# Fox gate sums from 64 keys to a partition, and low parts on GpSimd at the start of the feed-forward network

## The chip, the cores and the metric

One core of one Trainium2 chip runs the whole program. The time is that of one execution on the device, in microseconds. The engines are TensorE (PE, matmuls), VectorE (DVE), ScalarE (ACT), GpSimd (POOL) and SyncE (SP). In this kernel SP does no arithmetic: it issues every DMA, one after the other, in a fixed order.

## The reference

The reference is one step of a hybrid encoder layer: 1024 rows of a new stream (prompt) and 16 new rows for each of 8 running streams (decode), 1152 rows of width 1024 in all. Cut to what the change touches:

```python
logf = log_sigmoid(fg + fox_b_f)                      # one gate per row and head, 4 heads
fcum = cumsum(logf, axis=1)                           # prompt
fcum = cumsum(concat([past_fox_logf, logf]), axis=1)  # decode: 1024 cached gates, then 16 new
s = q @ k.T * 64 ** -0.5 + (fcum_q[:, None] - fcum_k[None, :])
p = softmax(where(k_pos <= q_pos, s, -inf))           # fox attention
...
hdn = silu(u @ w_gate) * (u @ w_up)                   # FFN, 1024 -> 2816
h = h + hdn @ w_down
```

Fox is one of three mixers that run side by side (stick-breaking attention, fox attention, a state-space scan). An output projection, a cross attention, the FFN and a final norm follow. Everything is float32.

## The kernel before

A float32 product is made of three matmuls of rounded parts. Every operand is split in a high part, rounded by ACT (`ACT.copy` into float32r), and a low part, the difference of the operand and its high part. The low part is made by DVE, or by POOL in pieces of 256 columns (`pool_tt`, L132).

**Order.** The program emits the work as interleaved generators. In the first half `pipeline` takes attention rows, and `fill_s` feeds projections, then `fox_sums`, between them. The framework's scheduler then sets the order on each engine by its own estimate of times. Each engine works its list in order, and SP's list holds all the DMAs.

**Fox sums.** `fox_sums` makes the new gates `lf` (a softplus, L396 to L411, 36 columns) and the prefix sums over the prompt (`fqc`, L676 to L680, with a matmul against a triangle of ones at L678). For decode it loads the cached gates with the key index on the partition: 128 partitions, 64 runs of 4 floats each (L666). It puts them in another order (L683), makes sums over the eight blocks of 128 keys (L693 to L696) and then fifteen matmuls of 128x32 by 128x128 (L708, L710), whose result, 32 rows (stream and head) by 1024 keys, goes through ACT (L711) to a scratch tensor in DRAM (L718), together with the 16 new gates' sums. Later each group of cached fox rows loads one scratch row to each partition (L909), and `fqs` takes the new gates' sums from it (L1246).

**Neighbours of the fox sums.** Cached keys come in pairs of 256 KB loads (`load_k`, L882) into a ring of four tiles `wr`, which the loads of `w_in` (L315) share. PE transposes them (L888), ACT copies them into `kf` (L890), and PE uses them at L873. ACT's cast L290 makes the high parts of `w_in`, POOL's L132 (`wl`) the low ones. Stick-breaking rows go through a DVE scan (L519) and a POOL product (L132, `ws`) before PE transposes them (L925, L577).

**FFN.** Gate and up projections are made tile by tile (22 tiles of 128 columns) as seven products of combined factors instead of eight plain ones. `left_factors(kt, eng)` loads the weights of one tile and makes the seven left factors, each with a high and a low part of 128x512 (`hi_lo`, L1689 on ACT, L1693 on DVE or L132 on POOL). `right_factors` makes the right factors of a group of rows from the transposed rows `u`: `put` writes high (L1753) and low part, and `sub` (L1697) is a difference on DVE, partly in place in `u`. Group 0 has 256 columns, and group 1 has 320 and is made in four pieces, one for each `kp`. At the start `gate_up` runs tile 0 on group 0, tile 1 on group 0, tile 1 on group 1, tile 0 on group 1, and then each further tile on both; `gen1` holds the left factors of tile 1. From tile 2 on, the low parts are on POOL. PE's FFN matmuls are at L1849, DVE's sums of results in PSUM at L1824.

## Time and profile before

| | us |
|---|---|
| median of 3 runs (lowest, highest) | 1916.93 (1914.52, 1922.89) |
| profiled execution | 1915.89 |
| its span | 1914.2 |
| busy: PE, DVE, ACT, POOL | 1837.6, 897.1, 823.7, 622.6 |

A row of the timeline has start, length, engine, line, operation, and what is written from what, with shapes. In square brackets stand the idle time of the engine before it and what ended this. "L882" is line 882 of the kernel before. The granted clock is that of PE as a share of full speed. The profiled execution took 1.7 us more than its span.

### The profile page before, as it was taken

To read this page: it belongs to the slowest core of one execution; us is meant where nothing else is said; L and a number is where in the kernel's file an instruction comes from. 1 tells how busy PE (TensorE), PEld (TensorE's weight loads), DVE (VectorE), ACT (ScalarE), POOL (GpSimd) and SP (SyncE) were. 2 spreads that over 40 slices of the span, in tenths; PEclk is the share of its full clock that TensorE was granted. 3 is DMA by queue.
4 is the path that set the end of the run, shared out by engine and by line. 5 is a ranking of instruction groups with operands and counts; after the bars stand their busy time and mean duration, and the time that the engine had idled before them with its cause. 6 is when DMAs were issued, how large, how long until landed. Compare 5 with 4: busy or idle time off the path is not lost. (4 is left out here: it accounts for less than half of the span.)

```text
span 1914.2 us, 32508 instructions
## 1 busy us (share of the span) xinstructions
PE 1837.6 (96%) x12146; PEld 1641.4 (86%) x12146; DVE 897.1 (47%) x1823; ACT 823.7 (43%) x1782; POOL 622.6 (33%) x921
## 2 busy tenths in 40 slices
PE   7989989999998889999999999999999999999998
PEld 5889877888876667898998889999999999888886
DVE  3421323457646873353445387333333433455554
ACT  6431534545566771243433275333333333344443
POOL 7532416254324563211102205544444443000000
PEclk9999998999999999999999999999999999999999
DMA  9455645536579887244558124322323223567572
GB/s 336 142 165 159 211 115 152 154 109 185 166 220 282 280 290 260 103 150 145 176 194 291 66 91 111 80 70 70 95 74 75 70 70 100 190 194 237 177 246 92
DMA packets 309742, 305.70 MB, mean 160 GB/s; under 512 B 89996, under 2 KB 261108, under 8 KB 309584
## 3 DMA queue, kind: packets, MB, share of 16 engines
q1 hardware_dynamic: 309584, 303.62, 51.6%
q8 instruction: 96, 1.57, 0.3%
q14 instruction: 62, 0.51, 0.1%
HBM read 229.31 MB, written 74.24 MB: 159 GB/s over the span
## 5 line engine op out<-in xcount | busy, mean ns | idle before, releaser
L132 POOL TENSOR_TENSOR wl<-wr,wh 128x256 fp32r<-128x256 f32 (+2 forms) x184 | 138.6, 787 | 222.4 <-ACT wh L290 202.0
L326 PE MATMUL psd<-act,wh 128*128 128x384 f32 x576 | 198.7, 345 | 5.1 <-DVE sg L453 2.7
L327 PE MATMUL psd<-act,wh 128*128 128x384 f32 x576 | 197.6, 343 | 0.0
L328 PE MATMUL psd<-act,wl 128*128 128x384 f32 x576 | 196.8, 342 | 0.7 <-POOL wl L132 0.7
L1849 PE MATMUL pst<-bT,tr 128*128 128x256 f32 (+1 forms) x1068 | 155.0, 293 | 0.0
L1849 PEld LDWEIGHTS pst<-bT,tr 128*128 128x128 f32 x1068 | 144.9, 188 | 0.1
L328 PE MATMUL psd<-wh,act 128*128 128x512 f32 (+3 forms) x424 | 135.8, 322 | 0.0
L326 PE MATMUL psd<-wh,act 128*128 128x256 f32 (+3 forms) x414 | 133.0, 324 | 2.4 <-ACT pt L1445 1.2
L1849 PE MATMUL psd<-bT,tr 128*128 128x320 f32 (+1 forms) x912 | 133.2, 295 | 0.8 <-DVE tr L1693 0.5
L327 PE MATMUL psd<-wl,act 128*128 128x256 f32 (+3 forms) x414 | 132.8, 322 | 0.5 <-POOL wl L132 0.5
L1849 PEld LDWEIGHTS psd<-bT,tr 128*128 128x128 f32 x912 | 124.7, 188 | 1.8 <-DVE tr L1693 0.7
L326 PEld LDWEIGHTS psd<-act,wh 128*128 128x128 f32 x576 | 109.1, 189 | 8.7 <-DVE sg L453 3.1
L132 POOL TENSOR_TENSOR tr<-u,tr 128x256 fp32r<-128x256 f32 x110 | 81.9, 774 | 102.3 <-ACT tr L1689 85.1
L328 PEld LDWEIGHTS psd<-act,wl 128*128 128x128 f32 x576 | 108.9, 189 | 2.3 <-POOL wl L132 1.0
L327 PEld LDWEIGHTS psd<-act,wh 128*128 128x128 f32 x576 | 109.0, 189 | 1.5 <-issue 1.1
L132 POOL TENSOR_TENSOR ws<-ws 128x256 f32<-128x256 f32 (+2 forms) x100 | 68.5, 713 | 115.3 <-DVE ws L519 99.9
L1824 DVE TENSOR_TENSOR tr<-tr,pst 128x256 f32<-128x256 f32 (+1 forms) x86 | 38.6, 449 | 139.5 <-ACT tr L1821 106.3
L251 POOL TENSOR_SCALAR sm<-sm 128x1 f32<-128x1 f32 (+2 forms) x27 | 7.1, 261 | 296.6 <-ACT y L1932 208.0
L132 POOL TENSOR_TENSOR tr<-raw,tr 128x256 fp32r<-128x256 f32 x94 | 69.2, 765 | 84.5 <-ACT tr L1689 76.3
L1689 ACT CAST tr<-tr 128x384 fp32r<-128x384 f32 (+1 forms) x70 | 37.7, 538 | 121.1 <-DMA tr<-hidsc 104.3
L290 ACT CAST wh<-wr 128x512 fp32r<-128x512 f32 (+2 forms) x90 | 52.2, 621 | 80.7 <-PE psd L328 31.0
L326 PEld LDWEIGHTS psd<-wh,act 128*128 128x128 f32 x414 | 78.3, 189 | 9.9 <-ACT pt L1445 1.5
(620 smaller groups left out, 4714.0 us busy)
## 6 DMA issues: line engine op xcount, KB each, us to landing
u<-w_down SPq DMA_DIRECT2D x40, 512.0 KB
raw<-w_down SPq DMA_DIRECT2D x26, 512.0 KB
st<-qksc SPq DMA_DIRECT2D x48, 256.0 KB
wr<-w_in SPq DMA_DIRECT2D x44, 256.0 KB
tr<-hidsc SPq DMA_DIRECT2D x57, 192.0 KB
hidsc<-tr SPq DMA_DIRECT2D x34, 288.0 KB
qksc<-sg SPq DMA_DIRECT2D x48, 192.0 KB
wr<-cache_sb_k SPq DMA_DIRECT2D x32, 256.0 KB
```

The source lines that it names most:

```text
L132: POOL.tensor_tensor(out=out[:, a0:a1], in0=in0[:, a0:a1], in1=in1[:, a0:a1], op=op)
L251: POOL.tensor_scalar(v, ss, inv, EPS, ALU.mult, ALU.add)
L290: ACT.copy(hi, raw)
L326: PE.matmul(out, ah, bh, start=start, stop=False)
L327: PE.matmul(out, ah, bl, start=False, stop=False)
L328: PE.matmul(out, al, bh, start=False, stop=stop)
L1689: ACT.copy(hi, src)
L1824: DVE.tensor_tensor(out=at(out, g), in0=at(x, g), in1=ps[g][:, :GW[g]], op=op)
L1849: PE.matmul(dst[g][:, :GW[g]], x[:, ka], y[:, k, :], start=start and k == 0 and m == 0, stop=stop and k == 3 and m == 2, skip_group_check= ...
```

## The change

In `fox_sums` the cached gates are loaded with 64 consecutive keys of one stream on a partition, 256 contiguous floats (16 partitions to a stream). Four scans on DVE, one for each head, sum along the 64 keys. The totals of the partitions are then summed over the earlier partitions of the same stream by a matmul with a mask (`before`, two more selects on POOL) and added. Two more small matmuls give the sums of the new gates and the streams' totals. The scratch tensor is laid out head by stream by key, and the new gates' sums have one of their own (`fn_sc`). The cached rows load it by two DMAs of 64 partitions instead of one of 128.

At the start of the FFN the low part of the right factor `T1`, in the four pieces of group 1, and the seven low parts of tile 1's left factors go from DVE to POOL.

```diff
     mix_sc = dram([8, 2, P, T], F32R, "mixsc")
     o_sc = dram([8, 2, P, T], F32R, "osc")
     fc_sc = dram([4, SEQ], F32, "fcsc")
-    fs_sc = dram([32, 2, PAST + DEC_S], F32, "fssc")
+    fs_sc = dram([4, DEC_B, PAST], F32, "fssc")
+    fn_sc = dram([32, DEC_S], F32, "fnsc")
     ac_sc = dram([72, P], F32, "acsc")
     mk_sc = dram([256, D], F32, "mksc")
     mv_sc = dram([256, D], F32, "mvsc")
...
         SP.dma_start(out=a["p_fox_logf"][0, 0].rearrange("(k p) h -> p k h", p=P), in_=lf[:, 0:8, :])
         SP.dma_start(out=a["s_fox_logf"][0].rearrange("b q h -> (b q) h"), in_=lf[:, 8, :])
 
-        pl0, pl1 = sg_t(), sg_t()
-        SP.dma_start(out=pl0[:, :256].rearrange("p (u h) -> p u h", h=4),
-                     in_=a["cache_fox_logf"][0].rearrange("b k h -> (b k) h").rearrange("(u p) h -> p u h", p=P))
-        triu, ones = pl1[:, 256:384], pl1[:, 384:512]
-        POOL.memset(pl1[:, 256:], 1.0)
+        lp, tri = sg_t(), sg_t()
+
+        SP.dma_start(out=lp[:, :256], in_=a["cache_fox_logf"][0].rearrange("b (c k) h -> (b c) (k h)", k=64))
+        triu, ones, before = (tri[:, i * P:(i + 1) * P] for i in range(3))
+        POOL.memset(tri[:, :384], 1.0)
         POOL.affine_select(out=triu, in_=triu, compare_op=ALU.is_ge, fill=0.0, base=0, pattern=[[1, P]],
                            channel_multiplier=-1)
+
+        b3 = before.rearrange("p (b t) -> p b t", t=16)
+        POOL.affine_select(out=b3, in_=b3, compare_op=ALU.is_ge, fill=0.0, base=-1, pattern=[[16, 8], [1, 16]],
+                           channel_multiplier=-1)
+        POOL.affine_select(out=b3, in_=b3, compare_op=ALU.is_ge, fill=0.0, base=0, pattern=[[-16, 8], [0, 16]],
+                           channel_multiplier=1)
 
         pre = sg2_t()
         DVE.tensor_copy(pre[:, 4:8], lf[:, 0, :])
...
         PE.matmul(tp[:, :32], triu, lf[:, 0:8, :].rearrange("p b h -> p (b h)"), start=True, stop=False)
         PE.matmul(tp[:, 4:32], ones, pre[:, 4:32], start=False, stop=True)
         DVE.tensor_copy(fqc.rearrange("p b h -> p (b h)"), tp[:, :32])
-
-        pp, ps_ = pl1[:, :256], pl0[:, 256:]
-        DVE.tensor_copy(pp.rearrange("p (k b h) -> p k b h", k=8, h=4),
-                        pl0[:, :256].rearrange("p (b k h) -> p k b h", k=8, h=4))
         yield
         fr = xc_t()
         for hf in range(2):
...
                 PE.transpose(tp[:4, b * P:(b + 1) * P], fqc[:, 4 * hf + b, :], ident)
             ACT.copy(fr[0:4, hf * 512:(hf + 1) * 512], tp[:4])
         SP.dma_start(out=fc_sc, in_=fr[0:4, :SEQ])
-        DVE.tensor_copy(ps_[:, 32:64], pp[:, 0:32])
-        for k in range(1, 7):
-            sl = slice(32 * k, 32 * k + 32)
-            DVE.tensor_tensor(out=ps_[:, 32 * k + 32:32 * k + 64], in0=ps_[:, sl], in1=pp[:, sl], op=ALU.add)
-        x8 = sg2_t()
-        DVE.tensor_tensor(out=x8[:, :32].rearrange("p (b h) -> p b h", h=4),
-                          in0=lf[:, 8, :].unsqueeze(1).to_broadcast([P, 8, 4]),
-                          in1=smask.unsqueeze(2).to_broadcast([P, 8, 4]), op=ALU.mult)
+
+        for hd in range(4):
+            x = lp[:, hd:256:4]
+            DVE.tensor_tensor_scan(lp[:, 256 + 64 * hd:320 + 64 * hd], x, x, 0.0, ALU.add, ALU.bypass)
+        tot = pre[:, 32:36]
+        DVE.tensor_copy(tot, lp[:, 319:512:64])
+        x8, t8 = pre[:, 64:96], pre[:, 96:128]
+        for out, src in ((x8, lf[:, 8, :]), (t8, tot)):
+            DVE.tensor_tensor(out=out.rearrange("p (b h) -> p b h", h=4), in0=src.unsqueeze(1).to_broadcast([P, 8, 4]),
+                              in1=smask.unsqueeze(2).to_broadcast([P, 8, 4]), op=ALU.mult)
         yield
-
-        sr = xc_t()[0:32, :PAST + DEC_S]
-        for hf in range(2):
-            tp = pd()
-            for k in range(4 * hf, 4 * hf + 4):
-                o = tp[:32, (k % 4) * P:(k % 4 + 1) * P]
-                PE.matmul(o, pp[:, k * 32:(k + 1) * 32], triu, start=True, stop=k == 0)
-                if k:
-                    PE.matmul(o, ps_[:, k * 32:(k + 1) * 32], ones, start=False, stop=True)
-            ACT.copy(sr[:, hf * 512:(hf + 1) * 512], tp[:32])
         tp = pd()
-        PE.matmul(tp[:32, :16], x8[:, :32], fold, start=True, stop=True)
-        ACT.copy(x8[0:32, 64:80], tp[:32, :16])
-        n8 = x8[0:32, 64:80]
+        PE.matmul(tp[:, :4], before, tot, start=True, stop=True)
+        PE.matmul(tp[:32, 16:32], x8, fold, start=True, stop=True)
+        PE.matmul(tp[:32, 32:48], t8, ones[:, :16], start=True, stop=True)
+        DVE.tensor_tensor(out=lp[:, 256:512].rearrange("p (h k) -> p h k", h=4),
+                          in0=lp[:, 256:512].rearrange("p (h k) -> p h k", h=4),
+                          in1=tp[:, 0:4].unsqueeze(2).to_broadcast([P, 4, 64]), op=ALU.add)
+
+        n8 = pre[0:32, 128:144]
+        DVE.tensor_copy(n8, tp[:32, 16:32])
         DVE.tensor_tensor_scan(n8, n8, n8, 0.0, ALU.add, ALU.bypass)
-        DVE.tensor_scalar(sr[:, PAST:], n8, sr[:, PAST - 1:PAST], None, ALU.add)
-        SP.dma_start(out=fs_sc, in_=sr.unsqueeze(1).to_broadcast([32, 2, PAST + DEC_S]))
+        DVE.tensor_tensor(out=n8, in0=n8, in1=tp[:32, 32:48], op=ALU.add)
+        SP.dma_start(out=fs_sc.rearrange("h b (c k) -> (b c) h k", k=64),
+                     in_=lp[:, 256:512].rearrange("p (h k) -> p h k", h=4))
+        SP.dma_start(out=fn_sc, in_=n8)
         yield
         y8 = sg2_t()
         DVE.tensor_tensor(out=y8[0:32, :P].rearrange("p (b t) -> p b t", t=DEC_S),
-                          in0=sr[:, PAST:].unsqueeze(1).to_broadcast([32, 8, DEC_S]),
+                          in0=n8.unsqueeze(1).to_broadcast([32, 8, DEC_S]),
                           in1=bmask32.unsqueeze(2).to_broadcast([32, 8, DEC_S]), op=ALU.mult)
         tp = pd()
         PE.matmul(tp[:, :P], hsel, y8[0:32, :P], start=True, stop=True)
...
             if m == 0:
                 return sb_rows(T, pieces), hold
             fkb = xc_t()
-            SP.dma_start(out=fkb[:, :PAST],
-                         in_=fs_sc[8 * p:8 * p + 8, :, :PAST].rearrange("i c k -> (i c) k").unsqueeze(1)
-                         .to_broadcast([16, DEC_S // 2, PAST]))
+            for b2 in range(2):
+                SP.dma_start(out=fkb[64 * b2:64 * b2 + 64, :PAST],
+                             in_=fs_sc[:, 2 * p + b2, :].unsqueeze(1).to_broadcast([4, DEC_S, PAST]))
             return fox_rows(T, pieces, [(0, PAST, fkb[:, :PAST]), (PAST, P, fnew)], fqs[:, p:p + 1]), hold
 
         def av(p, w, hold):
...
             if o == "z1":
                 for p in range(4):
                     tc.keep_in_program_order(
-                        SP.dma_start(out=fqs[:, p:p + 1], in_=fs_sc[8 * p:8 * p + 8, 0, PAST:PAST + DEC_S]))
+                        SP.dma_start(out=fqs[:, p:p + 1], in_=fn_sc[8 * p:8 * p + 8, :]))
             if o[0] == "z":
                 yield from z_proj(int(o[1]))
             elif o == "dt":
...
 
         kk, cc = slice(kps[0], kps[-1] + 1), slice((b0 - GB[g]) * 64, (b0 - GB[g] + n) * 64)
 
-        def put(two, src):
+        def put(two, src, eng=DVE):
             hi, lo = (t[:, :, kk, cc] for t in B[two, g])
             ACT.copy(hi, src)
-            sub(lo, src, f32(hi))
+            if eng is POOL and len(kps) == 1:
+                pool_tt(lo[:, 0, 0], src[:, 0, 0], f32(hi)[:, 0, 0], ALU.subtract)
+            else:
+                sub(lo, src, f32(hi))
         put(("11", "21"), u[:, :, 0])
         sub(u[:, :, 0], u[:, :, 1], u[:, :, 0])
         yield
-        put(("T1",), u[:, 0:1, 0])
+        put(("T1",), u[:, 0:1, 0], POOL)
         sub(u[:, 1, 0], u[:, 1, 0], u[:, 0, 0])
         yield
         put(("T4", "22"), u[:, 1])
...
     trp = ctx.enter_context(f_pool("trp", NR, "right"))
     slots.append((trp, "tr"))
     turn[0] = -1
-    gen1 = left_factors(1, DVE)
+    gen1 = left_factors(1, POOL)
 
     def step1(i):
         next(rgt, None)
```

The scheduler also moves neighbours. Two places of the fox sums and one of the FFN are shown, of the kernel before and then of the change, whose lines are one to seven higher. First SP, from the load of the cached gates on (`wr` are the ring's tiles, `lf` the new gates):

```order
L666 DMA sg<-cache_fox_logf 128x64x4
L882 DMA wr<-cache_sb_k 128x512 x2
L608 DMA mixsc<-sg 64x2x256
L882 DMA wr<-cache_sb_k 128x512 x2
L662 DMA p_fox_logf<-lf 128x8x4
L663 DMA s_fox_logf<-lf 128x4
L315 DMA wr<-w_in 128x2x256
L315 DMA wr<-w_in 128x2x8
```

```order
L668 DMA sg<-cache_fox_logf 128x256
L885 DMA wr<-cache_sb_k 128x512 x2
L609 DMA mixsc<-sg 64x2x256
L885 DMA wr<-cache_sb_k 128x512 x2
L316 DMA wr<-w_in 128x2x256
L316 DMA wr<-w_in 128x2x8
...
L316 DMA wr<-w_in 128x2x256
L663 DMA p_fox_logf<-lf 128x8x4
L664 DMA s_fox_logf<-lf 128x4
```

The load of the gates has another shape and keeps its place. The stores of the new gates, which stood ahead of all the loads of `w_in`, now stand behind seven of them.

At the same time, ACT (`kf` are the copied keys, `wh` the high parts of `w_in`, `pt` transposed attention weights):

```order
L517 ACTIVATE ws<-pss 128x512
L890 COPY kf<-pst 128x2x256 x4
L290 CAST wh<-wr 128x528
L580 COPY pt<-pst 128x512
L691 COPY xc<-psd 4x512
```

```order
L518 ACTIVATE ws<-pss 128x512
L893 COPY kf<-pst 128x2x256 x3
L581 COPY pt<-pst 128x512
L291 CAST wh<-wr 128x528
L893 COPY kf<-pst 128x2x256
L581 COPY pt<-pst 128x512
```

The fourth copy of keys now stands behind the first cast of `w_in`, and one copy of transposed weights ahead of it. DVE there, from the end of an attention unit on (`sg` are small work tiles, `so` too):

```order
L450 TENSOR_TENSOR sg<-so,sg 64x256
L402 TENSOR_SCALAR sg<-sg 128x36
L403 RECIPROCAL sg<-sg 128x36
L404 TENSOR_TENSOR sg<-sg 128x36
L405 TENSOR_TENSOR sg<-sg 128x36
L406 TENSOR_SCALAR sg<-sg 128x36
```

```order
L451 TENSOR_TENSOR sg<-so,sg 64x256
L699 SCALAR_TENSOR_TENSOR sg<-sg 128x64 x4
L403 TENSOR_SCALAR sg<-sg 128x36
L701 COPY so<-sg 128x4
L404 RECIPROCAL sg<-sg 128x36
L704 TENSOR_TENSOR so<-so,smask 128x32
L405 TENSOR_TENSOR sg<-sg 128x36
L406 TENSOR_TENSOR sg<-sg 128x36
```

The four scans over the cached gates (L699) stand ahead of the steps of the softplus (L402 before, L403 now) that make the new gates, and two small steps on the totals between these.

The start of the FFN, POOL (`tr` and `tl` hold left factors, `raw` the loaded weights, `bT` right factors):

```order
L251 TENSOR_SCALAR sm<-sm 128x1
L252 TENSOR_TENSOR sm<-sm,mhalf 128x1
L132 TENSOR_TENSOR tl<-raw,tl 128x256 x2
L132 TENSOR_TENSOR tr<-raw,tl 128x256 x2
L132 TENSOR_TENSOR tr<-raw,tr 128x256 x2
L132 TENSOR_TENSOR tr<-tr 128x256 x2
```

```order
L252 TENSOR_SCALAR sm<-sm 128x1
L253 TENSOR_TENSOR sm<-sm,mhalf 128x1
L132 TENSOR_TENSOR bT_12275<-u,bT_12274 128x256
L132 TENSOR_TENSOR bT_12275<-u,bT_12274 128x64
L132 TENSOR_TENSOR tr<-raw,tr 128x256 x2
L132 TENSOR_TENSOR bT_12275<-u,bT_12274 128x256
L132 TENSOR_TENSOR bT_12275<-u,bT_12274 128x64
L132 TENSOR_TENSOR tr<-raw,tr 128x256 x2
L132 TENSOR_TENSOR bT_12275<-u,bT_12274 128x256
L132 TENSOR_TENSOR bT_12275<-u,bT_12274 128x64
L132 TENSOR_TENSOR tr<-raw,tr 128x256 x2
L132 TENSOR_TENSOR tr<-tr 128x256 x2
```

Ahead of the first low parts that POOL made before (`tl`, tile 0 for its second use) it now has those of tile 1 and of T1, in pieces of 256 and 64 columns. On DVE the rows at L1693 (now L1696) for tile 1 and four rows of 128x320 at L1697 (now L1700) are gone; the differences in place are left.

## The prediction

> **What bounds the kernel now.** I read the page first, then TensorE's time in windows, then its idle gaps in the timeline and what ended them.
>
> ```profile
> PE 1837.6 (96%) x12146; PEld 1641.4 (86%) x12146; DVE 897.1 (47%) x1823; ACT 823.7 (43%) x1782; POOL 622.6 (33%) x921
> ```
>
> TensorE (PE) is busy 1837.6 of 1914.2 us, so the end moves only with work that PE loses, waits that it loses, or time at a lower clock. No other engine is near its limit over the span; VectorE (DVE) is, in one stretch. The change touches three stretches, and each has its own limit.
>
> The first is the fox sums. Columns: stretch, its length, busy time of each engine with its count, then granted clock, DMA share, GB/s:
>
> ```profile
> 278.00:281.00 3.00, 1.06 (x8) 0.16 (x8) 1.96 (x9) 1.95 (x6) 0.00 (x0) 1.00 0.65 19
> 281.00:284.00 3.00, 0.00 (x0) 0.00 (x0) 1.82 (x9) 0.24 (x1) 0.60 (x2) 0.72 1.18 90
> 284.00:287.00 3.00, 2.00 (x10) 2.03 (x10) 1.88 (x15) 0.61 (x2) 0.00 (x0) 0.50 0.98 297
> 287.00:290.00 3.00, 2.44 (x12) 2.24 (x13) 0.19 (x1) 1.15 (x2) 0.00 (x0) 0.50 1.00 125
> 290.00:293.00 3.00, 3.00 (x17) 2.24 (x16) 0.00 (x0) 1.10 (x2) 0.00 (x0) 0.58 0.56 136
> 302.00:305.00 3.00, 0.27 (x1) 0.27 (x2) 2.96 (x5) 0.37 (x2) 3.00 (x3) 0.63 0.85 241
> 305.00:308.00 3.00, 3.00 (x12) 2.61 (x12) 0.42 (x1) 1.19 (x3) 1.66 (x5) 0.50 0.01 5
> ```
>
> PE stands still twice, and after each time it runs at half clock. Its timeline shows what it waited for, in square brackets, and SP's shows why:
>
> ```profile
> 285.00 1.94 PE L888 MATMUL pst<-ident,wr 128*128 128x128 f32 x8 [4.91 <-DMA wr<-cache_sb_k]
> 287.52 1.09 PE L888 MATMUL pst<-ident,wr 128*128 128x128 f32 x4 [0.32 <-DMA wr<-cache_sb_k]
> 289.11 1.09 PE L888 MATMUL pst<-ident,wr 128*128 128x128 f32 x4 [0.24 <-DMA wr<-cache_sb_k]
> 304.73 1.13 PE L925 MATMUL pst<-ident,ws 128*128 128x128 f32 x4 [3.50 <-POOL ws L132]
> ...
> 276.99 0.45 SPq L666 DMA_DIRECT2D sg<-cache_fox_logf  x1
> 277.54 5.25 SPq L882 DMA_DIRECT2D wr<-cache_sb_k  x2
> 283.56 1.02 SPq L882 DMA_DIRECT2D wr<-cache_sb_k  x2
> ...
> DMA packets 8350, 0.27 MB, mean 48 GB/s; under 512 B 8224, under 2 KB 8344, under 8 KB 8350
> ...
> L882 SPq DMA_DIRECT2D wr<-cache_sb_k x32: 327/349/4777, 165.3 to 436.6; - x32
> ...
>   PE pst L888: 8.1, 5
> ```
>
> The packet row is for 277.5 to 283: 8,350 packets carry 0.27 MB. They are the 8,192 runs of 16 bytes of L666. The next issue, L882, holds SP for 4.78 us where its median is 0.35, and the keys that PE needs come late. PE's waits on them sum to 4.91 + 0.32 + 0.24 = 5.47 us. The last row counts PE's waits for all 64 key loads of that line: five, with 8.1 us, so undisturbed loads are nearly always in time.
>
> The second is the start of the feed-forward network (FFN):
>
> ```profile
> 1140.00:1150.00 10.00, 6.91 (x44) 5.92 (x43) 9.97 (x20) 7.59 (x17) 0.00 (x0) 0.79 0.12 26
> 1150.00:1160.00 10.00, 9.29 (x54) 8.22 (x53) 10.00 (x17) 8.33 (x17) 0.00 (x0) 0.87 0.19 55
> ...
> 1145.41 0.51 PE L1849 MATMUL psd<-b,tr 128*128 128x256 f32 x2 [1.62 <-ACT tr L1689]
> 1148.18 2.50 PE L1849 MATMUL psd<-b,tr 128*128 128x256 f32 x10 [1.09 <-DVE tr L1693]
> 1159.22 1.44 PE L1849 MATMUL psd<-bT,tr 128*128 128x256 f32 x10 [0.47 <-DVE tr L1693]
> ```
>
> Here DVE has no idle time for 20 us, and PE waits for it. GpSimd (POOL) does nothing. Better feeding could recover at most these gaps, 1.62 + 1.09 + 0.47 = 3.2 us, and the lower clock, 6.91 × 0.21 + 9.29 × 0.13 = 2.7 us.
>
> The third, the cached fox rows, has no PE gap where the gate loads land:
>
> ```profile
> 518.00:528.00 10.00, 10.00 (x84) 9.26 (x83) 5.20 (x16) 4.21 (x10) 3.86 (x11) 1.00 0.99 273
> 525.66 1.15 ACT L529 ACTIVATE ws<-xc,fqs 128x1024 f32<-128x1024 f32 x1 [3.97 <-DMA xc<-fssc]
> L909 SPq DMA_DIRECT2D xc<-fssc x4: 536/546/676, 520.2 to 630.1; - x4
> ```
>
> **The change part by part: the fox sums.** The gates now come as 128 runs of 1 KB instead of 8,192 of 16 bytes. L882's first pair should then issue in its usual 0.35 us each. So the keys come 4 to 5 us sooner, and the second pair, which SP issues behind the first and one store, as well. PE is ready at 280.09 (285.00 − 4.91). The two waits for such loads elsewhere are 8.1 − 5.47 = 2.6 us, 1.3 each. I leave 0.8 us, between nothing and 1.3: **−4.7** (−5.5 to −4).
>
> Half clock: from 284 to 293 PE is busy 2.00 + 2.44 + 3.00 = 7.44 us at 0.50, 0.50 and 0.58. At full clock this is 1.00 + 1.22 + 1.74 = 3.96 us, so at most 3.5 are lost. I take **−2.5** (−3.3 to −1), as the wait before it shortens but does not vanish. The row for 281 to 284 shows the clock falling inside the 4.91 us gap, and the FFN window shows 0.79 though its longest gap is 1.62 us. The Trainium skill, "TensorE: Matmul & The Clock Gate", in its part on the clock gate, says that the array drops to half after an idle window of about 3.4 us. By that rule a wait of 0.8 us leaves the clock alone, and this term would be −3.5. The 0.79 of the FFN window speaks against so clean a limit.
>
> Matmuls: fifteen go, in two passes each, and so do their ACT copies; three small ones come:
>
> ```profile
> L708 PE MATMUL psd<-sg x16: 272/273/297, 294.9 to 298.9; 128*32 128x128 f32 x16
> L710 PE MATMUL psd<-sg x14: 272/272/273, 295.3 to 299.2; 128*32 128x128 f32 x14
> ```
>
> They start 0.11 us apart (2.4 us from 294.9 to 297.2, 0.9 from 298.4 to 299.2), so 3.3 us go. The three new ones have 4, 16 and 16 columns, two passes each, some 0.7 us: **−2.6**.
>
> The wait at 304.73 is for POOL, which shares something with DVE there:
>
> ```profile
> 301.72 4.58 POOL L132 TENSOR_TENSOR ws<-ws 128x256 f32<-128x256 f32 x5
> L132 POOL TENSOR_TENSOR ws<-ws x3: 632/636/2365, 301.7 to 304.6; 128x256 f32<-128x256 f32 x3
> 301.63 2.02 DVE L519 TENSOR_TENSOR_SCAN ws<-ws 128x896 f32<-128x896 f32 x1 [1.30 <-ACT so L714]
> ...
> 292.48 0.63 ACT L290 CAST wh<-wr 128x528 fp32r<-128x528 f32 x1 [1.66 <-DMA wr<-w_in]
> ```
>
> The pair overlaps for the whole scan, and the one POOL piece in it takes 2.37 us instead of 0.64. The scan stays, but ACT reaches its inputs without the two 32x512 copies, and POOL can start earlier. The wait is 3.50 us, and half clock behind it costs 3.00 × 0.5 = 1.5 more; I take a third of it: **−1.5** (−4 to 0).
>
> Against that stand two new orders. On ACT the fourth key copy (L890) now follows the first cast of w_in (L290), which waited 1.66 us for its load: **+1.0** (0 to 2). On DVE the four scans, which need the gate load, now stand ahead of the softplus that makes the new gates. Behind them are lf, PE's L678 and the prefix: **+0.5** (0 to 2). The two extra selects of POOL and DVE's small adds lie in idle time of both (POOL 0.00 busy in four of the windows above); without that cover some 1 us.
>
> Sum of this stretch: −4.7 − 2.5 − 2.6 − 1.5 + 1.0 + 0.5 = −9.8; I use **−9** (−12 to −4), as gains that follow each other overlap a little.
>
> **The cached rows.** Four more issues of 0.55 us on SP, for the same bytes, and PE is 10.00 of 10 busy while ACT waits 3.97 us for such a load: **0** (±1.5).
>
> **The FFN start.** Seven low parts of 128x512 and four of 128x320 leave DVE. Rows for one with and without POOL beside it:
>
> ```profile
> 1148.44 0.69 DVE L1693 TENSOR_TENSOR tr<-raw,tr 128x512 fp32r<-128x512 f32 x1
> 1149.04 0.69 DVE L1705 TENSOR_TENSOR tr<-raw 128x512 f32<-128x512 f32 x1
> 1153.59 0.49 DVE L1697 TENSOR_TENSOR bT<-u,bT 128x320 fp32r<-128x320 f32 x1
> 1181.56 1.22 DVE L1697 TENSOR_TENSOR u<-u 128x512 f32<-128x512 f32 x1
> ...
> 1168.42 1.44 POOL L132 TENSOR_TENSOR tl<-raw,tl 128x256 fp32r<-128x256 f32 x2 [35.61 <-PE pso L1849]
> 1182.20 1.87 POOL L132 TENSOR_TENSOR tr<-u,tr 128x256 fp32r<-128x256 f32 x2
> ```
>
> DVE starts its 128x512 operations 0.60 us apart and those of 320 columns 0.40, so it is rid of 7 × 0.60 + 4 × 0.40 = 5.8 us. But beside POOL the 0.69 us operation takes 1.22: 0.53 us are lost to one piece of POOL. The change puts 14 whole pieces and 4 whole with 4 short ones into the very stretch in which DVE is full: 18 × 0.53 + 4 × 0.2 (a quarter of a piece) = 10.3 us. DVE ends 4.5 us worse, not 5.8 better. The low part itself takes 1.44 to 1.87 us on POOL instead of 0.69 on DVE. And DVE's in-place steps now wait for POOL: the update of u for T1, and those of a11 and a12, each with all of DVE behind it. PE waits for DVE at 1148.18, which gets better by up to 1.09 as POOL is free at once, and at the third factor and 1159.22, which get worse by DVE's 4.5. Net at PE 3.4, taken as **+3**: no less than −3.5 (both DVE gaps, 1.56, and most of the 2.7 of clock, with no loss by overlap), no more than +6 (4.5 and a clock that falls by as much again as the 1.2 us of 1150 to 1160).
>
> The Trainium skill, "SBUF — State Buffer", section "Who interferes with whom", says more: the pair of ports is locked for the whole instruction, whoever comes first. Read strictly, each piece of 0.72 us stops DVE fully, 18 × 0.72 + 4 × 0.2 = 13.8 us against 5.8. By that DVE is 8 us later, and this term +8 or more. The row of 1.22 us agrees that they exclude each other, but shows 0.53 lost.
>
> Total: 1915.9 (the profiled execution) − 9 + 0 + 3 = 1909.9. The median of the runs shown is 1 us above the profiled one; I say **1910**.
>
> **The rivals.**
>
> *Both parts gain.* POOL's pieces fall between DVE's operations that read PSUM or wait, and the FFN start gives −3 instead of +3. For it: POOL is idle for 35.61 us. Against: DVE is 10.00 of 10 busy. With fox at −9 to −10 this is 1903.5. Chance 0.22.
>
> *The storm was hidden.* PE's gap at 285 passes to the next thing that is late: the w_in casts, or the gates' own chain on DVE, so the fox part gives only −4 to −5; with +3 behind it about 1914.5. For it: ACT already waits 1.66 us for w_in, and the clock stays low. Against: those loads also stood behind the storm. Chance 0.15.
>
> *The lock eats more than the gates give.* This is the other side. If a piece stops DVE for all of its 0.72 us (1.44 for two), DVE is 8 us late, PE waits that long at the third and the later factors, and its clock, 0.87 over these 9.29 busy us, falls to about 0.55, which costs another 3: +11 against −9, so 1918. It decides from a loss L per piece with 18 × L + 0.8 − 5.8 = 9, that is 0.78 us, or 0.61 with the clock's 3. Measured is 0.53. Chance 0.08.
>
> That the change does not do what it says I leave out: the new instructions are plainly in the program.
>
> **How the numbers follow.** The forecast has 0.55. Its own range is 1906 to 1914. The range for 8 in 10 goes from **1903** (most of the first rival) to **1917** (the second and part of the third). A difference of 0.5% or 9.6 us is about what a measurement of this kernel can tell from none. Faster by more, under 1907.3, takes a fifth of the forecast and most of the first rival: 0.55 × 0.2 + 0.22 × 0.85 = **0.30**. Slower by more needs 1926, the far end of the third: **0.03**. The rest is **0.67**.
>
> **What would show it.** Right: in the changed profile PE's gap at L888 is near 1 us, no issue at the key loads lasts over 1 us, and the clock from 281 to 290 stays above 0.8; and at the FFN start DVE stays full past 1157, with its 128x512 operations at 1.0 to 1.2 us beside POOL's, and PE waits for the third factor. Wrong: a gap of several us at L888 with another releaser, or DVE done early with operations at 0.69. If PE's gaps in both stretches shrink and the time does not, a wait further on took them, against the gapless stretch after 310.

## The result: 1.1% slower

The kernel before has a median of 1914.78 us (6 runs, 1913.19 to 1922.89) and the changed one 1937.85 us (6 runs, 1933.47 to 1941.35). The ratio is 1.0111, with a 95% interval of 1.0088 to 1.0134. The forecast was 1910 us in a range of 1903 to 1917, so it had the wrong sign. The profiled execution of the changed kernel took 1939.98 us, with a span of 1938.2 us, 24.0 us longer than before. Two of the twelve executions of one later kernel (the one with 16 source rows to a load) took 2998.92 and 3667.77 us at a granted clock of 0.56 and 0.51, and are left out of its numbers.

Where the 24 us come from is read from the same matmul in both traces. Rows of PE's timeline (start, length, engine, line, operation, and in brackets the wait before it), of the kernel before:

```profile
279.02 1.06 PE L873 MATMUL pss<-kf,st 128*32 128x512 f32 x8 [1.21 <-ACT kf L890]
309.71 0.62 PE L785 MATMUL psd<-ident,xc 24*128 24x24 f32 x8
491.77 0.27 PE L760 MATMUL psd<-ident,so 128*27 128x128 f32 x1 [0.99 <-DVE so L756]
593.99 0.63 PE L888 MATMUL pst<-ident,wr 128*128 128x128 f32 x4 [2.35 <-DMA wr<-cache_fox_k]
684.62 0.67 PE L1055 MATMUL psd<-ident,act 128*128 128x128 f32 x4 [3.01 <-DMA act<-xbcsc]
1632.22 0.40 PE L326 MATMUL psd<-tr 128*128 128x512 f32 x1
1653.98 0.50 PE L326 MATMUL psd<-tr 128*128 128x512 f32 x1 [1.11 <-ACT tr L1689]
```

and of the changed kernel:

```profile
279.81 1.06 PE L876 MATMUL pss<-kf,st 128*32 128x512 f32 x8 [1.21 <-ACT kf L893]
301.82 0.99 PE L788 MATMUL psd<-ident,xc 24*128 24x24 f32 x8
490.00 0.27 PE L763 MATMUL psd<-ident,so 128*27 128x128 f32 x1 [1.35 <-DVE so L759]
607.35 1.09 PE L891 MATMUL pst<-ident,wr 128*128 128x128 f32 x4 [7.26 <-DMA wr<-cache_fox_k]
702.58 0.63 PE L1058 MATMUL psd<-ident,act 128*128 128x128 f32 x4 [2.53 <-DMA act<-xbcsc]
1164.31 0.51 PE L1855 MATMUL psd<-b,tr 128*128 128x256 f32 x2 [1.62 <-ACT tr L1692]
1655.05 0.40 PE L327 MATMUL psd<-tr 128*128 128x512 f32 x1
1677.83 0.50 PE L327 MATMUL psd<-tr 128*128 128x512 f32 x1 [2.14 <-ACT tr L1692]
```

The rows at 1632.22 and 1655.05 are the first products of w_down, the next two a product of w_down further on. With the first FFN matmul before (1145.41), the changed kernel stands behind by these amounts:

| stretch | behind at its start | behind at its end | the stretch costs |
|---|---|---|---|
| fox sums and what follows, 279 to 490 us | +0.8 | −1.8 | −2.6 |
| cached fox rows, 490 to 703 us | −1.8 | +18.0 | +19.7 |
| rest of attention, to the first FFN matmul | +18.0 | +18.9 | +0.9 |
| FFN, to the first product of w_down | +18.9 | +22.8 | +3.9 |
| w_down, to the product at 1653.98 | +22.8 | +23.9 | +1.0 |

So 19.7 of the 24 us lie in the one stretch that the prediction costed at nothing.

### The profile page after: what moved, and what is told of

It reads as the page before. It is cut to its first block, busy times and chain, and to the rows that moved or that the text cites. A ratio compares the mean times of both kernels' runs of the same rounds, so it can differ in the third digit from the quotient of the medians.

```text
span 1938.2 us, 32487 instructions
## 1 busy us (share of the span) xinstructions
PE 1843.4 (95%) x12120; PEld 1644.0 (85%) x12120; DVE 894.9 (46%) x1812; ACT 823.5 (42%) x1779; POOL 648.8 (33%) x945
## 4 chain that ended last, share of the span: by engine, by line
PE 77%; DMA 8%; POOL 5%; DVE 4%; issue 3%; ACT 3%; SPq 1%; POOLq 0%; DVEq 0%; ACTq 0%
PE psd L1855 10%; PE psd L327 9%; PE psd L328 9%; PE psd L329 9%; PE pst L1855 8%; PE pss L1855 3%; PE pss L327 3%; PE pss L328 3%; PE pss L329 3%; POOL wl L132 2%; PE pso L1855 2%; PE pst L327 1%; PE pst L328 1%; PE pst L329 1%; PE pso L593 1%
## 5 line engine op out<-in xcount | busy, mean ns | idle before, releaser
L132 POOL TENSOR_TENSOR tr<-raw,tr 128x256 fp32r<-128x256 f32 x106 | 82.4, 805 | 89.1 <-ACT tr L1692 81.0
L328 PEld LDWEIGHTS psd<-wl,act 128*128 128x128 f32 x414 | 79.7, 193 | 8.7 <-POOL wl L132 2.2
```

The costliest lines, as they stand in the source:

```text
L132: POOL.tensor_tensor(out=out[:, a0:a1], in0=in0[:, a0:a1], in1=in1[:, a0:a1], op=op)
L328: PE.matmul(out, ah, bl, start=False, stop=False)
```

## The profile after

**The cached fox rows.** ACT, DVE and PE in the timeline of the changed kernel:

```profile
530.71 1.15 ACT L530 ACTIVATE ws<-xc,fqs 128x1024 f32<-128x1024 f32 x1 [10.77 <-DMA xc<-fssc]
532.46 0.36 ACT L416 ACTIVATE so<-psd 128x256 f32<-128x256 f32 x1
...
532.85 0.42 DVE L417 SCALAR_TENSOR_TENSOR sg<-so,psd 128x256 f32<-128x256 f32 x1 [9.39 <-ACT so L416]
...
533.32 0.58 PE L327 MATMUL psd<-wh,act 128*128 128x256 f32 x1 [6.69 <-DVE sg L417]
```

The issues of these loads, grouped by line (count, then min, median and max ns, and the first and last start):

```profile
L913 SPq DMA_DIRECT2D xc<-fssc x8: 533/557/4954, 518.5 to 644.4; - x8
```

ACT waits 10.77 us for the gates' sums, where it waited 3.97 before. Behind this wait on ACT stands L416, a copy out of the PSUM tile of the z projection. DVE waits for that copy, and PE for the tile. The matmuls that had covered the shorter wait have run out, and PE stands for 6.69 us. One of the eight issues, at 593.25, holds SP for 4.95 us. Three loads of cached keys stand right behind it on SP (598.31), and PE's wait for cached keys (L888 before, L891 now) goes from 2.35 to 7.26 us.

The whole stretch as one window, before and changed (columns as in the prediction):

```profile
491.77:684.62 192.85, 173.01 (x1381) 139.15 (x1381) 132.15 (x382) 127.79 (x285) 76.25 (x127) 0.98 0.78 235
490.00:702.58 212.58, 180.08 (x1380) 144.90 (x1381) 129.19 (x380) 127.77 (x285) 75.63 (x126) 0.93 0.71 212
```

Of the 19.7 us, 12.7 are idle time of PE (32.50 against 19.84), and 7.1 are longer busy time for the same matmuls, at a mean clock of 0.93 instead of 0.98.

What the DMA engines did just after the first two of these loads were issued, from 521 to 523 us, changed kernel and then before (packets, MB, and the queue's time as a share of 16 engines):

```profile
DMA packets 143, 0.19 MB, mean 94 GB/s; under 512 B 0, under 2 KB 111, under 8 KB 143
q1 hardware_dynamic: 143, 0.19, 34.6%
```

```profile
DMA packets 417, 0.66 MB, mean 330 GB/s; under 512 B 48, under 2 KB 304, under 8 KB 417
q1 hardware_dynamic: 417, 0.66, 105.0%
```

In these 2 us only a third of the DMA engines' time is used, where the kernel before used all of it. A little later, from 522.5 to 524.5 us, other transfers bring the share to 99.4%, so the share alone does not tell how this load is moved. The start and length of each packet in the trace tell more. Of the packets of 4 KB, the size of one row of the scratch tensor, 3.7 are under way at a time in the mean from 521 to 527 us, and for most of the time exactly 4.

**The fox sums.** Windows of the changed kernel (columns as in the prediction):

```profile
285.00:288.00 3.00, 2.58 (x24) 1.50 (x21) 0.67 (x5) 2.77 (x7) 1.54 (x3) 1.00 0.87 220
291.00:294.00 3.00, 1.26 (x10) 0.76 (x8) 1.07 (x1) 1.92 (x6) 1.38 (x3) 0.97 0.71 206
294.00:297.00 3.00, 3.00 (x14) 1.99 (x11) 2.45 (x4) 2.95 (x8) 3.00 (x4) 0.50 1.00 257
303.00:306.00 3.00, 3.00 (x15) 3.00 (x16) 1.54 (x4) 1.15 (x3) 3.00 (x5) 0.50 0.19 44
```

In its timeline, the waits of PE and ACT, and POOL's pieces:

```profile
281.27 1.26 PE L891 MATMUL pst<-ident,wr 128*128 128x128 f32 x8 [0.40 <-DMA wr<-cache_sb_k]
283.77 1.00 PE L891 MATMUL pst<-ident,wr 128*128 128x128 f32 x5 [1.24 <-DMA wr<-cache_sb_k]
292.08 0.63 ACT L291 CAST wh<-wr 128x528 fp32r<-128x528 f32 x1 [2.62 <-DMA wr<-w_in]
293.11 0.44 PE L560 MATMUL pss<-st 128*128 128x384 f32 x1 [1.74 <-ACT ws L518]
299.64 1.13 PE L928 MATMUL pst<-ident,ws 128*128 128x128 f32 x4 [1.93 <-POOL ws L132]
296.63 9.76 POOL L132 TENSOR_TENSOR ws<-ws 128x256 f32<-128x256 f32 x9
```

The waits for keys fell from 5.47 to 1.64 us, and the clock from 285 to 288 is 1.00 instead of 0.50. But ACT now waits for the last piece of w_in, PE waits for ACT, and half clock comes from 294 us on, when POOL is busy without a gap. In the kernel before, half clock held from 282 to 292 and again from 303 us on. At the 24x24 matmuls PE stands 309.71 − 301.82 = 7.9 us ahead of the kernel before, and at 490 us 1.8: of what was won by 302 us, 6 us are given back by 490. Half clock until 307.5 costs 2 to 3 of these 6 us (an estimate: PE is busy throughout, at a clock of 0.50 from 302 to 306 and 0.75 from 306 to 309). Two waits for ACT that the kernel before does not have, 0.43 us at 317.64 and 1.29 at 320.81, are another 1.7. The rows do not share out the rest.

**The FFN start.** PE's next waits behind the row of 1164.31:

```profile
1165.69 1.70 PE L1855 MATMUL psd<-b,tr 128*128 128x256 f32 x10 [0.87 <-POOL tr L132]
1169.64 0.62 PE L1855 MATMUL pss<-b,tr 128*128 128x256 f32 x3 [2.02 <-POOL tr L132]
```

POOL's low parts of the left factors as one group (min, median, max ns):

```profile
L132 POOL TENSOR_TENSOR tr<-raw,tr x6: 734/1242/1318, 1164.3 to 1177.3; 128x256 fp32r<-128x256 f32 x6
```

A piece of POOL takes 1.24 us in the median, where the shortest takes 0.73, and PE's longest wait there is for POOL.

## The experiments: the loads of the gates' sums

Theory E was formed on the two traces: a load whose source is 4 rows, each copied to 16 partitions, is moved by few of the 16 DMA engines. The kernel before kept every row twice in its scratch tensor, so that its load had 16 source rows, each copied to 8 partitions. The rivals are the number of issues (I) and the scheduler's moves (S).

**The changed kernel with 16 source rows to a load.**

```diff
-    fs_sc = dram([4, DEC_B, PAST], F32, "fssc")
+    fs_sc = dram([4, 4, DEC_B, PAST], F32, "fssc")
...
-        SP.dma_start(out=fs_sc.rearrange("h b (c k) -> (b c) h k", k=64), ...)
+        for i in range(4):
+            SP.dma_start(out=fs_sc[:, i].rearrange("h b (c k) -> (b c) h k", k=64), ...)
...
             for b2 in range(2):
                 SP.dma_start(out=fkb[64 * b2:64 * b2 + 64, :PAST],
-                             in_=fs_sc[:, 2 * p + b2, :].unsqueeze(1).to_broadcast([4, DEC_S, PAST]))
+                             in_=fs_sc[:, :, 2 * p + b2, :].rearrange("h i k -> (h i) k").unsqueeze(1)
+                             .to_broadcast([16, DEC_S // 4, PAST]))
```

> The changed kernel, with the scratch tensor of the cached gates' sums written four times (four DMAs instead of one) and each load of 64 partitions taken from 16 source rows, each copied to 4 partitions, instead of from 4 rows, each copied to 16. Number of loads, their bytes and everything else stay. Theory E (few source rows): a load from four rows is moved by few of the 16 DMA engines, which costs some 20 us between 520 and 750; then this kernel has 1917 to 1920 us, no gap of 6.7 us near 527, and the first load lands within 6 us. Theory I (more issues): the second DMA of each group and SP's time are the cause; then it stays at 1936 to 1940. Theory S (order): the neighbours that the scheduler moved are the cause; then also about 1938, unless the order is moved again.

Measured: 1916.14 us, ratio to before 0.9995 (0.9973 to 1.0017). No loss against the kernel before is left that can be told, with the same number of loads and three stores more. The wait on ACT:

```profile
525.71 1.15 ACT L530 ACTIVATE ws<-xc,fqs 128x1024 f32<-128x1024 f32 x1 [4.72 <-DMA xc<-fssc]
```

4.72 us against 10.77 and, before the change, 3.97. I falls, as the loads are still eight; S falls with the next run.

**The kernel before with 4 source rows to a load.**

```diff
-            SP.dma_start(out=fkb[:, :PAST],
-                         in_=fs_sc[8 * p:8 * p + 8, :, :PAST].rearrange("i c k -> (i c) k").unsqueeze(1)
-                         .to_broadcast([16, DEC_S // 2, PAST]))
+            for b2 in range(2):
+                r0 = 8 * p + 4 * b2
+                SP.dma_start(out=fkb[64 * b2:64 * b2 + 64, :PAST],
+                             in_=fs_sc[r0:r0 + 4, 0, :PAST].unsqueeze(1).to_broadcast([4, DEC_S, PAST]))
```

> The kernel before, with each load of the cached gates' sums split in two of 64 partitions, each from 4 source rows copied to 16 partitions; nothing else changes. E: slower by 15 to 22 us, 1930 to 1937, with the DMA share falling to a quarter while the two loads run alone. I: the same 1930 to 1937. S: 1915, as no other part of the change is there.

Measured: 1940.76 us, 1.0118 (1.0087 to 1.0150). This edit alone brings the whole loss of the change, and a little more than the 15 to 22 us expected.

**The kernel before with 8 source rows to a load.**

```diff
-                         in_=fs_sc[8 * p:8 * p + 8, :, :PAST].rearrange("i c k -> (i c) k").unsqueeze(1)
-                         .to_broadcast([16, DEC_S // 2, PAST]))
+                         in_=fs_sc[8 * p:8 * p + 8, 0, :PAST].unsqueeze(1).to_broadcast([8, DEC_S, PAST]))
```

> The kernel before, with each load of the cached gates' sums still one DMA of 128 partitions, but from 8 source rows copied to 16 partitions instead of 16 rows copied to 8. E: half of the DMA engines move it, so it lands some 9 to 10 us after its issue instead of 5.5, and the kernel is slower by 5 to 12 us, 1920 to 1927. I: the number of issues is that of before, so 1915. S: 1915.

Measured: 1925.10 us, 1.0028 (1.0009 to 1.0048). With the same number of issues as before it is slower, by some 5 us, so I and S cannot be the cause here. ACT's wait in this kernel and in the one with 4 rows:

```profile
533.83 1.15 ACT L529 ACTIVATE ws<-xc,fqs 128x1024 f32<-128x1024 f32 x1 [8.43 <-DMA xc<-fssc]
```

```profile
533.11 1.15 ACT L529 ACTIVATE ws<-xc,fqs 128x1024 f32<-128x1024 f32 x1 [11.05 <-DMA xc<-fssc]
```

With 16, 8 and 4 source rows ACT waits 3.97, 8.43 and 11.05 us. ACT's wait also depends on when ACT gets there, so here is the time from SP's first issue of the load to the start of the ACT operation that waits for it:

| kernel | source rows | issue | ACT starts | between, us |
|---|---|---|---|---|
| before | 16 | 520.17 | 525.66 | 5.5 |
| changed, 16 rows | 16 | 519.49 | 525.71 | 6.2 |
| before, 8 rows | 8 | 524.05 | 533.83 | 9.8 |
| before, 4 rows | 4 | 520.55 | 533.11 | 12.6 |
| changed | 4 | 518.53 | 530.71 | 12.2 |

The packets agree. Of those of 4 KB, 4.1 are under way at a time in the mean with 4 rows (522.8 to 528 us) and 8.3 with 8 rows (527 to 530 us). With 16 rows there are 14.3 before and 13.5 in the changed kernel (522 to 523 us); packets of another load may be among these.

The Trainium skill has this as a rule: "DMA: Bandwidth & Descriptors", section "Why a DMA increments its semaphore by 16 and not by 1", says that a DMA is spread over the largest number of engines, up to 16, that divides the outermost dimension of both of its access patterns. For these loads the rule gives 16, 8 and 4 engines, and the waits and the number of packets under way agree. The traces show how many packets run at a time, not which engine moves them.

## The experiments: the FFN start

The stretch is measured from the first FFN matmul to the first product of w_down, as in the table above: 486.8 us before (1145.41 to 1632.22), 490.7 in the changed kernel. In the run above with 16 source rows it is 490.0. It repeats well: in the seven other profiles of this document whose FFN start is that of before, it is 486.7 to 486.8.

**Both moves alone, on the kernel before** (`put` for T1 with POOL, and `gen1 = left_factors(1, POOL)`, as in the change).

> The kernel before with only the second part of the change: low parts of T1 in group 1 and of tile 1's left factors on GpSimd. Theory of the prediction (VectorE loses about 0.5 us to each GpSimd piece): 3 to 5 us slower, 1917.5 to 1920, with PE's waits at the second product of tile 1 and at the third factor. Rival (GpSimd is free and VectorE full, so PE is fed sooner): 2 to 4 us faster. Rival (whole lock): 10 us slower.

Measured: 1920.04 us, 1.0008 (0.9989 to 1.0027). As a time this is no difference. The stretch is 489.9 us, 3.1 longer than before, as the theory has it; neither rival fits. But PE's longest waits there, 0.88 and 1.47 us at 1146.46 and 1150.40, are for POOL's pieces, as in the changed kernel, and not for a DVE that is late.

**Tile 1's left factors alone.**

```diff
-    gen1 = left_factors(1, DVE)
+    gen1 = left_factors(1, POOL)
```

> The kernel before with only the seven low parts of tile 1's left factors on GpSimd (T1's stay on VectorE). Read by PE's progress between 1140 and 1190 alone, as one time tells less than 5 us. Theory (VectorE loses half a microsecond to each of 14 pieces, and gets back 4.2): PE 1 to 4 us later there. Rival (T1's pieces, which the update of u waits for, are what costs): 0 to 2 us sooner.

Measured in the one profile: a time of 1922.16 us, and a stretch of 493.2 us, 6.4 longer, where 1 to 4 were expected, and more than both moves together. PE waited 7.58 us for one piece of POOL. It was run again, with the long piece as the question.

> The kernel of the run with only tile 1's left factors on GpSimd once more, with times and another profile. There one GpSimd piece of 128x256 took 8.01 us, while VectorE ran operation after operation at its full pace, and PE waited 7.58 us for it. Theory H (a VectorE that is always ready again keeps GpSimd out until it stops): the same piece is again 5 to 10 us long, and the kernel 4 to 8 us slower. Rival (a mishap of one execution): all pieces are 0.7 to 1.4 us, and the kernel within 3 us of before.

Measured: 1924.28 us, 1.0045 (1.0030 to 1.0060), with a stretch of 493.2 us once more. POOL's pieces in this profile (min, median, max ns):

```profile
L132 POOL TENSOR_TENSOR tr<-raw,tr x4: 721/726/8009, 1153.2 to 1162.5; 128x256 fp32r<-128x256 f32 x4
```

The window around the long one:

```profile
1150.00:1160.00 10.00, 2.01 (x14) 1.37 (x13) 10.00 (x18) 5.77 (x13) 6.84 (x1) 0.75 0.13 27
```

Two of DVE's operations in it, and PE's wait:

```profile
1153.68 0.82 DVE L1697 TENSOR_TENSOR b<-u,b 128x640 fp32r<-128x640 f32 x1
...
1158.36 0.82 DVE L1697 TENSOR_TENSOR bT<-u,bT 128x640 fp32r<-128x640 f32 x1
...
1161.22 1.65 PE L1849 MATMUL psd<-b,tr 128*128 128x256 f32 x6 [7.59 <-POOL tr L132]
```

Again a piece of 8.01 us. DVE is busy for 10.00 of these 10 us, as it was before, and its 128x640 operations both take 0.82 us. POOL's piece does not end while this lasts. So it is no mishap, and for this piece H holds. As a rule H is not shown. In the run with both moves DVE is as full in the same window, and POOL's pieces of left factors get in:

```profile
1150.00:1160.00 10.00, 9.04 (x46) 8.10 (x46) 10.00 (x13) 7.76 (x16) 5.73 (x7) 0.78 0.17 45
L132 POOL TENSOR_TENSOR tr<-raw,tr x9: 982/1305/1341, 1145.1 to 1164.6; 128x256 fp32r<-128x256 f32 x9
```

There the two share the harm: POOL's pieces take up to 1.34 us, and DVE's 128x640 operations up to 1.36 instead of 0.82. What decides between the two cases is open.

**T1 alone** (`put` with an `eng` as in the change).

```diff
-        put(("T1",), u[:, 0:1, 0])
+        put(("T1",), u[:, 0:1, 0], POOL)
```

> The kernel before with only T1's low parts (four of 128x320, in pieces of 256 and 64) on GpSimd; the left factors of tile 1 stay on VectorE. Read by PE's progress between 1140 and 1190. By the prediction's price (0.7 us lost for each, 0.4 saved): 0.5 to 2 us later. If the left factors alone are the cost: 0.

Measured: 1919.90 us, 1.0023 (1.0008 to 1.0038), with a stretch of 491.5 us, 4.7 longer. That is more than twice what was expected. T1's low parts are nearly as dear as the left factors, and the two together cost less than either. One reading is that DVE's update of u waits for T1's piece, and that this pause lets the left factors' pieces in (8.01 us without T1's waits, 1.24 in the median with them). No run isolates it, and in the window above DVE has no pause at all.

## The experiments: the fox sums

**The kernel before without the 16-byte packets.**

```diff
-        SP.dma_start(out=pl0[:, :256].rearrange("p (u h) -> p u h", h=4),
-                     in_=a["cache_fox_logf"][0].rearrange("b k h -> (b k) h").rearrange("(u p) h -> p u h", p=P))
+        SP.dma_start(out=pl0[:, :256], in_=a["cache_fox_logf"][0].rearrange("b (c k) h -> (b c) (k h)", k=64))
```

> The kernel before, with the cached gates loaded as 128 runs of 1 KB into the same tile; the sums then add the wrong gates, so the decode rows of fox are not the reference's. Matmuls, order and stores are those before. The prediction's terms for the packets and for the clock behind them (4.7 and 2.5 us): PE's gap of 4.91 us at the keys falls to about 1 and its clock stays over 0.8 from 281 to 290, so PE is 6 to 8 us ahead at 293; it then keeps 3 to 8 of them, 1909 to 1914. Rival (keys late for another reason): the gap stays over 3 us, and 1917.

Measured: 1917.66 us, 1.0005 (0.9991 to 1.0018). PE's waits:

```profile
281.05 0.63 PE L887 MATMUL pst<-ident,wr 128*128 128x128 f32 x4 [0.28 <-DMA wr<-cache_sb_k]
281.93 0.63 PE L887 MATMUL pst<-ident,wr 128*128 128x128 f32 x4 [0.25 <-DMA wr<-cache_sb_k]
284.64 1.00 PE L887 MATMUL pst<-ident,wr 128*128 128x128 f32 x5 [2.09 <-DMA wr<-cache_sb_k]
294.66 0.65 PE L592 MATMUL pso<-pt,st 128*64 128x256 f32 x4 [2.00 <-ACT pt L580]
```

The waits for keys are 0.28 + 0.25 + 2.09 = 2.62 us instead of 5.47, and the clock is 1.00 from 281 to 296 us. So the gap of 4.91 us and the half clock behind it were the packets' doing, as predicted, though 2.09 us is more than the 1 expected. PE is 3.8 us ahead at the 24x24 matmuls (305.87 against 309.71) and 1.9 behind at the first FFN matmul (1147.27 against 1145.41): nothing of it is left in the time. The prediction's terms were right where they stood, and the step from them to the end was not.

**The changed kernel with 16 source rows and the FFN part undone.** Edits as above, and `put` and `gen1` as before.

> The changed kernel with loads of the cached gates' sums from 16 source rows (scratch written four times) and without the second part (the low parts at the start of the FFN are back on VectorE). Against the run with only the first of these, 3 to 4 us faster, by the trace's own count between 1140 and 1180; against the kernel before 1 to 5 us faster, 0.998 to 0.9995. If the FFN part cost nothing there, it stands level with that run.

Measured: 1913.36 us, 0.9986 (0.9974 to 0.9999). The run with the FFN part has 0.9995 (0.9973 to 1.0017), so the two times do not tell these kernels apart. The traces do: the stretch is 486.8 us here, 3.3 shorter. PE's waits:

```profile
294.10 0.44 PE L560 MATMUL pss<-st 128*128 128x384 f32 x1 [2.26 <-ACT ws L518]
302.81 1.13 PE L930 MATMUL pst<-ident,ws 128*128 128x128 f32 x4 [4.92 <-POOL ws L132]
```

The wait for POOL, 3.50 us before, is 4.92 here: PE comes there 3.3 us earlier than before (297.89 against 301.23), POOL's piece only 1.9 (302.81 against 304.73).

**The new gates' stores behind the sums' stores**, on top of that.

```diff
-        SP.dma_start(out=a["p_fox_logf"][0, 0].rearrange("(k p) h -> p k h", p=P), in_=lf[:, 0:8, :])
-        SP.dma_start(out=a["s_fox_logf"][0].rearrange("b q h -> (b q) h"), in_=lf[:, 8, :])
...
         SP.dma_start(out=fn_sc, in_=n8)
         yield
+        tc.keep_in_program_order(SP.dma_start(out=a["p_fox_logf"][0, 0]..., in_=lf[:, 0:8, :]))
+        tc.keep_in_program_order(SP.dma_start(out=a["s_fox_logf"][0]..., in_=lf[:, 8, :]))
```

> As the run without the second part, and the two stores of the new gates (1,152 packets of 16 bytes) stand behind the stores of the sums instead of ahead of the last load of w_in. Theory G (what the fox sums give back after 300 us is the wait for that load behind the store's 16-byte packets, and the half clock after it): ACT's wait of 2.6 us at the fourth cast and PE's gap of 1.7 us are gone, the gain at 310 us stays at 6 to 8 us, and the kernel is 2 to 4 us faster than without this. Rival (VectorE's scans and GpSimd's products hold each other up there anyhow): PE waits 2 to 4 us at the transposes of stick-breaking weights instead, and nothing is gained.

Measured: 1909.21 us, 0.9964 (0.9952 to 0.9977). The wait for ACT at 294 us is gone from PE's rows, and the one for POOL stays:

```profile
303.78 1.13 PE L930 MATMUL pst<-ident,ws 128*128 128x128 f32 x4 [4.76 <-POOL ws L132]
```

The time speaks for G, the profile for its rival, so it was timed again.

> The kernel with 16 source rows to a load, without the second part and with the new gates' stores late, timed again on another occasion, since its first five times (median 1909.21) lie 4 to 5 us under those of the runs with and without its neighbours' changes, and PE's progress in its trace does not show why. If the lateness of the stores is worth 4 us: 0.995 to 0.998 again, and PE's progress from 900 us on 4 us or more ahead. If not: 0.9975 to 1.0 like the runs beside it.

Measured: 1907.87 us, 0.9958 (0.9942 to 0.9974). The gain is there again. This is the fastest kernel of the study, 8 us below the kernel before and some 30 below the changed one. Where the 4 to 5 us against the run without late stores lie is not settled: the two profiles of the late kernel took 1912.65 and 1911.87 us, above their own medians, and the one of the other kernel 1910.74, below its median, and PE's positions in them do not differ by that much.

**Low parts of z's first weights on VectorE**, on top of that (`dense_N` passes an engine to `w_unit`, DVE for `z_proj(0)`).

> The kernel with 16 source rows to a load, without the second part and with the new gates' stores late, and the low parts of z's first weights (128x528, four of them, which GpSimd made from 290 to 300 us) on VectorE, which is idle there. Theory P (from 293 to 311 us GpSimd is the bound: low parts of w_in first, then the products ws that PE's transposes wait for, and each held up by VectorE's scans): PE's wait of 4.8 us at these transposes falls to 0 to 2 us, the half clock behind it goes, and the kernel is 3 to 7 us faster than the run before it, 1902 to 1907. Rival (the scans themselves are the bound): the wait moves less than 2 us, and 1908 to 1911.

Measured: 1914.01 us, 0.9994 (0.9980 to 1.0009), slower than without (0.9958, 0.9942 to 0.9974). PE's longest wait for POOL there, and two waits that were not in the run before:

```profile
296.68 1.13 PE L931 MATMUL pst<-ident,ws 128*128 128x128 f32 x4 [1.74 <-POOL ws L132]
317.64 1.08 PE L940 MATMUL pso<-vr,st 128*32 128x128 f32 x32 [2.14 <-DMA vr<-cache_sb_v]
322.40 1.10 PE L578 MATMUL pst<-ident,ws 128*128 128x128 f32 x7 [1.93 <-DVE so L451]
```

P is right about the wait (4.76 to 1.74) and wrong about the rest: half clock comes all the same, from 296 to 306 us, and the time is no better. At the 24x24 matmuls PE stands 8.3 us ahead of the kernel before (301.41 against 309.71), and at the first FFN matmul 3.3 (1142.12 against 1145.41). The two new waits, for values of the cache (`vr`) and for DVE, come to 4.1 us (2.14 + 1.93), against 5.0 lost between.

## Why the prediction was wrong, point by point

- **The cached rows, 0 (±1.5),** is the step that failed. It measured +19.7 us. Two things were wrong in it. It counted bytes and issues ("for the same bytes"), not how the load is spread over the DMA engines; and its cover, a PE busy for 10.00 of 10 us, was shown for a wait of 3.97 us, with no row for how much longer it would hold. It did not: at 10.77 us PE stood for 6.69, and with the wait for keys behind another of these loads (7.26) and the half clock after such waits the stretch lost 19.7. The three runs on the source rows show that their number is the cause. The change's own code (a source of 4 rows, copied 16 times, where 16 rows were copied 8 times) held all that was needed.
- **Waits for keys, −4.7:** 5.47 us became 1.64, so −3.8, just short of the term's range of −5.5 to −4. The run without the packets shows that they were the cause.
- **Half clock, −2.5:** from 285 to 288 us the clock is 1.00. Right in its place. But half clock came back from 294 us on and stayed until 307.5, which the term did not count.
- **The matmuls, −2.6, and the two new orders, +1.0 and +0.5:** not measured apart. ACT's wait for w_in went from 1.66 to 2.62 us, and PE has a new wait of 1.74 behind it.
- **The wait for POOL, −1.5:** 3.50 became 1.93 us in the changed kernel, but 4.76 to 5.42 in the four runs with 16 source rows that leave POOL's work there as it is, with and without the FFN part. Why these differ from the changed kernel no run shows.
- **The sum of the fox terms, −9 (−12 to −4), was the second step to fail.** It carried every gain to the end, but for a little overlap, and named a "gapless stretch after 310". The stretch from 279 to 490 us gave −2.6, outside the range. The next chains, ACT's casts, POOL's pieces and later loads, were only a few us behind PE.
- **The FFN start, +3:** +3.9 in the changed kernel, +3.2 with 16 source rows, +3.1 alone. Right in sign and size, but partly by luck. The term was built on a DVE that loses 0.53 us to each piece and is 4.5 us late for PE; PE's waits at 1165.69 and 1169.64 (0.87 and 2.02 us) are for POOL's own pieces. And the parts cost more apart (+6.4 and +4.7) than together, which no price per piece gives.
- **The rivals:** the second, that the gain of the sums is taken by what is late next, the w_in casts or the gates' chain, comes nearest to the run with 16 rows (0.9995); the wait for w_in is in the rows, but what else took the gain is not shown. None of the three had the loads of the cached rows, and the one that ended on the slower side put it in the FFN.
- **The signs:** PE's gap at the keys (1.24 us) and the clock there (1.00) are what the prediction named as signs of being right. They came true in a kernel that is 24 us slower, because the stretch that lost had no sign.

Without the slow loads the change gives 0.9995 of the time before (0.9973 to 1.0017), no difference that can be told; 1910 of 1916.93, the forecast, is 0.9964 and lies outside that interval.

## What to carry to other kernels

A load that is rewritten with a broadcast must be costed by the outermost dimension of its source, not by its bytes; 4 rows copied 16 times took 12.6 us from issue to use, 16 rows copied 8 times 5.5. A cover found for a wait of 4 us is no cover for one of 11, so a term of zero needs the length of its cover. And a wait removed on the engine that bounds is worth what the next chains leave: here 8 us at 302 us, and 2 us at 490.

## What the runs showed of the hardware that was not expected

- POOL was kept out for 8.01 us, in two executions, by a DVE that ran more than ten operations between SBUF tiles without a pause and at its full pace. With both moves, beside a DVE as full, POOL's pieces took at most 1.34 us. The Trainium skill, "SBUF — State Buffer", section "Who interferes with whom", has the lock held for a whole instruction. The runs agree that one is blocked; that it lasted over more than ten instructions in a row goes beyond what the section states.
- PE's clock halved after a gap of 1.74 us. From 290.38 to 293.79 us PE was busy for 1.67 of 3.41 us, and from 293.8 to 307.5 the clock is 0.50. In all the traces, from 100 to 1700 us, half clock comes in stretches of 3.4 us or of two, three or four times that. The prediction had weighed an idle window of 3.4 us from the Trainium skill, "TensorE: Matmul & The Clock Gate"; the lengths of the stretches agree with a window of 3.4 us, but the gap of 1.74 us does not fit an idle one.
